# Recurrent block of a two-layer trunk: a result block's two halves are multiplied together, and two recurrence blocks stand ahead of the first gate pair

## The chip, the cores and the metric

The kernel runs on one core of one Trainium2 chip. The metric is the device time of one launch in microseconds (us). The engines are TensorE (PE: matrix products, into the accumulator memory PSUM), VectorE (DVE), ScalarE (ACT), GpSimd (POOL) and SyncE (SP), whose queue issues the transfers. Each engine works through its own list in order; semaphores tie the lists together.

## What is computed

A trunk of two layers over 1024 tokens of width 1024: a recurrent block and a squared-ReLU MLP, then a chunked attention and another MLP. The change touches only the recurrent block:

```python
def recurrent_block(x, w_in, conv_w, conv_b, w_gate, b_gate, lam, w_out):
    u = x @ w_in                          # x is already RMS-normed
    gate, rec = u[..., :D_RNN], u[..., D_RNN:]
    rec = causal_depthwise_conv(rec, conv_w, conv_b)     # 4 taps
    h = rg_lru(rec, w_gate, b_gate, lam)
    return (jax.nn.gelu(gate) * h) @ w_out

def rmsnorm(x, g):
    y = xf * lax.rsqrt(jnp.mean(xf * xf, axis=-1, keepdims=True) + EPS)
    return (y * g.astype(jnp.float32)).astype(x.dtype)
```

`rg_lru` makes, for each of 8 groups of 128 channels, two gates (`sigmoid` of a 128 x 128 product each), from them a factor `a` and an input `b` per token, and runs h[t] = a[t] h[t-1] + b[t] along the tokens.

## The kernel before

**Layout.** Everything is held with channels on the 128 partitions and tokens along the row: 8 blocks of 128 channels by 1024 tokens. A product is done as three matmuls of 128 x 128 by 128 x 512 (`mm`, lines 335 to 337), high and low parts of both operands: wh*xh, wh*xl, wl*xh. So one result block of 128 channels by 1024 tokens over 8 blocks of input is 8 x 2 halves x 3 = 48 matmuls. It fills a tile `p` of PSUM, 128 x 1024 in fp32, whose two halves of 512 tokens are called 0 and 1 (`hs(h)`). There are four such tiles (`bank2`, counted by `pss`).

**The norm** of the input isn't applied ahead of the product. The product runs over x times the gain, and the result is multiplied by the root of each token, `R[0]` and `R[1]`, one for each half. That is line 598, on VectorE, in place in PSUM.

**The blocks.** r(n) is the block n of the recurrence's input, g(n) that of the gate, p(n) the pair of 128 x 128 gate products of recurrence block n (12 matmuls into two tiles). r0 and g0 run together at the start; then `order` (line 473) says what PE does: "r1 g1 p0 r2 p1 r3 p2 g2 r4 p3 g3 r5 p4 g4 r6 p5 r7 g5 p6 g6 p7 g7". In a block (`block`, line 701) PE does half 0 and half 1 over the first four input blocks, then half 0 and half 1 over the last four. Behind w_in's blocks come those of w_out ("out").

**The chains.** What follows a block is written as a Python generator:

- `conv(n)`, line 604: multiplies done, it takes a buffer `c`, forms the last tap on ScalarE (line 611), adds the other three on VectorE (line 618) and lets the tile `p` go; then it takes two buffers and splits `c` into `ch` and `cl` (lines 627, 629), which p(n) reads. From n = 2 on it first waits for `posted[n - 2]`.
- `lru(n)`, line 633, behind p(n): takes three buffers and sets `posted[n]`, sigmoids of both tiles (lines 640, 642, which let them go), tanh, line 648 on GpSimd (which lets `c` go), exp and one minus on ScalarE (653, 654), lines 656 to 664 on VectorE, 666 on GpSimd, and the scan, line 670, which sets `hidden[n]`.
- `gate(n)`, line 677, behind g(n): a buffer of another kind, the GELU (line 682, which lets the tile go), times the hidden state (687), and a split into the operands of w_out (693, 695).
- `split_half`, line 486, makes the high and low part of half a weight block (493 on ScalarE, 495 on VectorE) in ten tiles `w`, counted by `wss`; the weights with places 2 and 3 in the sequence (`IN_G`) take tiles of another pool. `worder` is that sequence: r0, g0, and then `order` without the pairs.

Buffers `c`, `ch`, `cl` and those of `lru` are of one kind; there are seven (`bs`). Those of `gate` and the result of `lru` are of another; there are four (`xs`).

**What sets the order.** The program of all engines is written in the order that a small model of time, `Plan`, finds when it is built. `Plan.pe` adds 512 columns at 2260 per us to PE's time, `Plan.use` a cost to another engine's; a generator yields a time, a `Flag` or a `Sema` and goes on when the plan's time has come there. What a generator calls is emitted at that moment, so the plan decides in what sequence each engine gets its instructions. The waits between engines are put in afterwards, from which instruction writes and reads which tile.

**The step of the change.** When `block` has emitted the last product of a half (`k == ks[-1]`), it starts `scale(ps, h, done)` for that half; `scale` waits for `normal[h]`, emits line 598 for that half and sets `done[h]`. `conv` and `gate` begin with `yield done[0]` and `yield done[1]`.

Of the kernel before, what the change touches and what calls it, by code (L numbers as in the profile page):

```python
# [13 lines left out]
ALU = mybir.AluOpType  # L14
# [4 lines left out]
NF = 8  # L19
H2 = 512  # L20
# [18 lines left out]
LAT = 0.3  # L39
# [119 lines left out]
def tile_yoco_rglru_chunk_attention(  # L159
# [17 lines left out]
    act, dve, pool, pe = nc.scalar, nc.vector, nc.gpsimd, nc.tensor  # L177
# [20 lines left out]
    def nm(s):  # L198
        cnt[0] += 1
        return f"{s}_{cnt[0]}"  # L200
# [10 lines left out]
    def bf(s="b", dt=F32):  # L211
        return bp.tile([P, T], dt, tag="b", name=nm(s))
# [25 lines left out]
    def hs(h):  # L238
        return slice(h * H2, (h + 1) * H2)
# [161 lines left out]
    plan = Plan(2260)  # L401
    R = [None, None]
    X = [[None, None] for _ in range(NF)]
# [46 lines left out]
    def d_(n):  # L450
        return 0.16 + n * 0.00106
# [6 lines left out]
    def flags(*shape):  # L458
        return {x: Flag(plan) for x in itertools.product(*(range(n) for n in shape))}
# [3 lines left out]
    normal, gained = flags(2), flags(1)  # L463
# [6 lines left out]
    goods = Sema(plan, 0)  # L470


    order = "r1 g1 p0 r2 p1 r3 p2 g2 r4 p3 g3 r5 p4 g4 r6 p5 r7 g5 p6 g6 p7 g7".split()
    order = [(x[0], int(x[1])) for x in order]
    worder = [NF, 0] + [n + NF * (kind == "r") for kind, n in order if kind != "p"]
    wsrc = [w_in[x] for x in worder] + [w_out[j] for j in range(NF)]
# [115 lines left out]
        dve.scalar_tensor_tensor(lo, x, g, hi.bitcast(F32), ALU.mult, ALU.subtract)  # L592
        parted[k, h].set(plan.use("dve", d_(H2)))

    def scale(ps, h, done):
        yield plan.now + LAT
        yield normal[h,]
        dve.tensor_tensor(ps[:, hs(h)], ps[:, hs(h)], R[h], ALU.mult)  # L598
        done.set(plan.use("dve", d_(H2)))

    def scales(ps, h, done):
        plan.start(scale(ps, h, done[h]))

    def conv(n, ps, done):
        yield done[0]
        yield done[1]
        if n >= 2:
            yield posted[n - 2,]
        yield bs
        c = bf("c")  # L610
        act.activation(
            c, ps, AF.Identity,
            scale=vec[:, V_CW + 3, n : n + 1], bias=vec[:, V_CB, n : n + 1],
        )
        yield plan.use("act", a_(T))
        for k in range(3):
            d = 3 - k
            dve.scalar_tensor_tensor(
                c[:, d:], ps[:, : T - d], vec[:, V_CW + k, n : n + 1], c[:, d:], ALU.mult, ALU.add
            )  # L620
            yield plan.use("dve", d_(T)) - LAT
        pss.release(plan.t + LAT)
        yield plan.t + LAT
        yield bs
        yield bs
        ch, cl = bf("ch", F32R), bf("cl", F32R)
        act.activation(ch, c, AF.Copy)
        yield plan.use("act", a_(T))
        dve.tensor_tensor(cl, c, ch.bitcast(F32), ALU.subtract)
        C[n] = c, ch, cl  # L630
        conved[n,].set(plan.use("dve", d_(T)))
# [42 lines left out]
        HID[n] = u  # L674
        hidden[n,].set(last)

    def gate(n, ps, done):
        yield done[0]
        yield done[1]
        yield xs  # L680
        g = xf("ge")
        act.activation(g, ps, AF.Gelu_apprx_tanh)
        last = plan.use("act", a_(T) + TABLE)
        pss.release(last)
        yield last
        yield hidden[n,]
        dve.tensor_tensor(g, g, HID[n], ALU.mult)
        last = plan.use("dve", d_(T))
        xs.release(last)
        yield last  # L690
        for h in range(2):
            hi, lo = gr("h"), gr("l")
            act.activation(hi, g[:, hs(h)], AF.Copy)
            yield plan.use("act", a_(H2))
            dve.tensor_tensor(lo, g[:, hs(h)], hi.bitcast(F32), ALU.subtract)
            Y[n][h] = (hi, lo)
        last = plan.use("dve", 2 * d_(H2))
        xs.release(last)
        out_y[n,].set(last)

    def block(ps, i, Z, ks, start, stop, done=None):
        ys = [[k for k in ks if k // 4 == y] for y in range(2)]
        for h, k in [(h, k) for mine in ys for h in range(2) for k in mine]:
            y = k // 4
            yield weighed[i, y]
            if Z is Y:
                yield out_y[k,]
            w = W[i, y]
            mm(
                ps[:, hs(h)], (w[0][:, k % 4, :], w[1][:, k % 4, :]), Z[k][h],  # L710
                start and k == ks[0], stop and k == ks[-1],
            )
            yield plan.pe(3 * H2) - LAT
            if i not in IN_G and h == 1 and k == ys[y][-1] and k % 4 == 3:
                wss.release(plan.now)
                wss.release(plan.now)
            if done and k == ks[-1]:
                scales(ps, h, done)

    def tensor():  # L720
        dones = [[Flag(plan), Flag(plan)] for _ in range(2 * NF)]
        pss_ = []
        for x in range(2):
            yield pss
            pss_.append(bank2())
        for h in range(2):
            for k in range(NF):
                for x in range(2):
                    yield weighed[x, k // 4]
                    yield parted[k, h]  # L730
                    w = W[x, k // 4]
                    ps = pss_[x]
                    mm(ps[:, hs(h)], (w[0][:, k % 4, :], w[1][:, k % 4, :]), X[k][h], k == 0, k == NF - 1)
                    yield plan.pe(3 * H2) - LAT
                    if k == NF - 1:
                        scales(ps, h, dones[x])
        for _ in range(8):
            wss.release(plan.now)
        plan.start(conv(0, pss_[0], dones[0]))
        plan.start(gate(0, pss_[1], dones[1]))  # L740
        allk = range(NF)
        for kind, n in order:
            if kind == "p":
                yield conved[n,]
                yield pss
                yield pss
                pair = []
                for e in range(2):
                    ps = bank2()
                    pair.append(ps)  # L750
                    gw, (c, ch, cl) = GW[n], C[n]
                    for h in range(2):
                        mm(ps[:, hs(h)], (gw[0][:, e, :], gw[1][:, e, :]), (ch[:, hs(h)], cl[:, hs(h)]), True, True)
                        yield plan.pe(3 * H2) - LAT
                bs.release(plan.now)
                bs.release(plan.now)
                wss.release(plan.now)
                plan.start(lru(n, *pair))
                continue
            yield pss  # L760
            ps = bank2()
            i = widx[n + NF * (kind == "r")]
            yield from block(ps, i, X, allk, True, True, dones[i])
            plan.start((conv if kind == "r" else gate)(n, ps, dones[i]))
        for _ in range(NG - 4 * NF - 4):
            goods.release(plan.now)
        plan.start(ahead_weights())
        ahead = {}
        for j in range(2):
            yield pss  # L770
            ahead[j] = bank2()
            yield from block(ahead[j], widx["out", j], Y, range(NF - 2), True, False)
        for j in range(2):
            yield from block(ahead[j], widx["out", j], Y, range(NF - 2, NF - 1), False, False)
        for j in range(NF - 2):
            if j in ahead:
                ps = ahead[j]
                yield from block(ps, widx["out", j], Y, range(NF - 1, NF), False, True)
            else:
                yield pss  # L780
                ps = bank2()
                yield from block(ps, widx["out", j], Y, allk, True, True)
            plan.start(o1.result(j, ps))

        last = {}
        for j in (NF - 2, NF - 1):
            yield pss
            last[j] = bank2()
        for k in allk:
            for j, ps in last.items():  # L790
                i = widx["out", j]
                yield weighed[i, k // 4]
                w = W[i, k // 4]
                for h in range(2):
                    mm(
                        ps[:, hs(h)], (w[0][:, k % 4, :], w[1][:, k % 4, :]), Y[k][h],
                        k == 0, k == NF - 1,
                    )
                    yield plan.pe(3 * H2) - LAT
                if k % 4 == 3:  # L800
                    wss.release(plan.now)
                    wss.release(plan.now)
                if k == NF - 1:
                    plan.start(o1.result(j, ps))
            for _ in range(4):
                goods.release(plan.now)
# [527 lines left out]
    X, R = o2.XS, o2.rr  # L1334
# [6 lines left out]
    plan = Plan()  # L1341
# [365 lines left out]
    with tc.manual_schedule(engines=set(ENG)) if ENG else ExitStack():  # L1707
# [3 lines left out]
        while True:  # L1711
            plan.flush()
            if begun < len(units) and filled >= due[begun] and rows.free(plan.now):
                n = units[begun]
# [19 lines left out]
    for j in range(JP):  # L1734
        for h in range(2):
            ps = bank()
# [73 lines left out]
```

## Time and profile before

| | us |
|---|---|
| median of 3 runs | 2137.61 (2136.71 to 2138.93) |
| the profiled execution | 2139.37 |
| span of the profile, first to last instruction | 2137.6 |

The page's busy digits, 40 equal slices of 53.4 us each (9 is 90% or more):

```profile
PE   9899999999999999999999999989999999999999
DVE  7777868877777776747777877777787777777743
ACT  7766635434344545546666666764543444444631
POOL 3222202333210000126656666650133332000000
```

The recurrent block is in the first six slices, up to 324 us, where the last product with w_out ends. In rows of the order of time there stand the start in us, the duration in us, engine, line, operation, out<-in; in brackets the idle time of the engine before it and what ended it. A matmul's row lasts 0.39 us though the next one starts 0.23 us after it, since matmuls are pipelined.

### The profile page before, as it was taken

How to read it: one execution, taken by the hardware profiler on the slowest of the kernel's cores; microseconds unless marked ns; L12 is line 12 of the kernel's file. 1: busy time of each engine (PE TensorE's matmuls, PEld its weight loads, DVE VectorE, ACT ScalarE, POOL GpSimd, SP SyncE). 2: the span in 40 equal slices, each digit the busy share in tenths (PEclk: the TensorE clock that was granted, in tenths of full speed). 3: DMA queues.
4: the chain of work that ended last, by engine and by line, in shares of the span. 5: the costliest groups of instructions: out<-in, count | busy, mean ns of one | idle time of the engine just before them, and what ended most of it. 6: DMA issues, size and time to landing. Idle time of an engine off the chain costs nothing.

```text
span 2137.6 us, 29379 instructions
## 1 busy us (share of the span) xinstructions
PE 2090.3 (98%) x9756; PEld 1729.4 (81%) x9756; DVE 1555.8 (73%) x2593; ACT 1102.3 (52%) x1964; POOL 592.5 (28%) x536
## 2 busy tenths in 40 slices
PE   9899999999999999999999999989999999999999
PEld 7677787888888888887888888878778888888887
DVE  7777868877777776747777877777787777777743
ACT  7766635434344545546666666764543444444631
POOL 3222202333210000126656666650133332000000
PEclk9999999999999999999999999999999999999999
DMA  4011334544469774534323333343364445987733
GB/s 161 30 38 45 118 104 158 177 157 155 150 233 315 240 257 129 165 117 110 87 73 97 91 91 83 86 155 124 103 215 144 158 153 173 332 260 243 243 107 94
DMA packets 174296, 319.21 MB, mean 149 GB/s; under 512 B 20544, under 2 KB 22592, under 8 KB 174144
## 3 DMA queue, kind: packets, MB, share of 16 engines
q1 hardware_dynamic: 174144, 317.33, 46.0%
q8 instruction: 77, 1.26, 0.3%
q14 instruction: 75, 0.61, 0.1%
HBM read 219.73 MB, written 78.64 MB: 140 GB/s over the span
## 4 chain that ended last, share of the span: by engine, by line
PE 86%; DVE 7%; ACT 3%; issue 2%; DMA 1%; POOL 1%; SPq 0%; DVEq 0%; POOLq 0%; ACTq 0%
PE pj L335 11%; PE pj L337 11%; PE pj L336 11%; PE tp L335 6%; PE tp L337 6%; PE tp L336 6%; PE sc L336 4%; PE sc L337 4%; PE sc L335 4%; PE p L335 3%; PE p L336 3%; PE p L337 3%; PE tp L1591 2%; PE po L1619 2%; PE po L1618 1%
## 5 line engine op out<-in xcount | busy, mean ns | idle before, releaser
L335 PE MATMUL pj<-h,wh 128*128 128x512 f32 x1198 | 481.3, 402 | 4.8 <-DVE s L1126 3.5
L336 PE MATMUL pj<-l,wh 128*128 128x512 f32 x1198 | 467.6, 390 | 0.7 <-POOL l L1644 0.7
L337 PE MATMUL pj<-h,wl 128*128 128x512 f32 x1198 | 467.8, 391 | 0.2
L1045 ACT ACTIVATE wh<-raw 128x512 fp32r<-128x512 f32 x349 | 218.9, 629 | 316.7 <-PE po L336 86.1
L1046 DVE TENSOR_TENSOR wl<-raw,wh 128x512 fp32r<-128x512 f32 x349 | 269.9, 776 | 103.3 <-ACT wh L1045 99.7
L335 PEld LDWEIGHTS pj<-h,wh 128*128 128x128 f32 x1198 | 225.7, 188 | 48.4 <-DVE s L1126 4.5
L337 PEld LDWEIGHTS pj<-h,wl 128*128 128x128 f32 x1198 | 224.9, 188 | 49.2 <-DVE wl L1046 1.0
L336 PEld LDWEIGHTS pj<-l,wh 128*128 128x128 f32 x1198 | 225.9, 189 | 38.9 <-POOL l L1644 1.4
L335 PE MATMUL tp<-h,wh 128*128 128x512 f32 x569 | 221.5, 389 | 0.0
L336 PE MATMUL tp<-l,wh 128*128 128x512 f32 x569 | 221.4, 389 | 0.0
L337 PE MATMUL tp<-h,wl 128*128 128x512 f32 x569 | 221.4, 389 | 0.0
L349 DVE TENSOR_TENSOR l<-raw,h 128x512 fp32r<-128x512 f32 x224 | 153.9, 694 | 29.7 <-ACT h L348 28.3
L335 PE MATMUL p<-h,wh 128*128 128x512 f32 x384 | 153.7, 400 | 21.6 <-DVE p L598 21.0
L348 ACT ACTIVATE h<-raw 128x512 fp32r<-128x512 f32 x224 | 137.4, 620 | 58.0 <-DMA raw<-hid 34.8
L336 PE MATMUL sc<-l,wh 128*128 128x512 f32 x425 | 166.0, 391 | 0.0
L337 PE MATMUL sc<-h,wl 128*128 128x512 f32 x425 | 165.9, 391 | 0.0
L335 PE MATMUL sc<-h,wh 128*128 128x512 f32 x425 | 165.6, 390 | 0.0
L1127 ACT ACTIVATE s<-s 128x512 f32<-128x512 f32 x125 | 78.3, 629 | 164.7 <-DVE s L1126 164.7
L1054 POOL TENSOR_TENSOR raw<-raw,raw 128x512 f32<-128x512 f32 x30 | 49.7, 1658 | 407.0 <-DVE wl L1046 399.7
L336 PE MATMUL p<-l,wh 128*128 128x512 f32 x384 | 151.7, 395 | 0.3 <-DVE l L592 0.2
L337 PE MATMUL p<-h,wl 128*128 128x512 f32 x384 | 151.3, 394 | 0.1
L295 POOL TENSOR_TENSOR raw<-raw,vec 128x512 f32<-128x512 f32 x48 | 54.2, 1130 | 262.3 <-DVE l L349 259.2
(276 smaller groups left out, 4224.6 us busy)
## 6 DMA issues: line engine op xcount, KB each, us to landing
raw<-hid SPq DMA_DIRECT2D x224, 256.0 KB, 3.6
hid<-s SPq DMA_DIRECT2D x221, 256.0 KB, 2.1
raw<-in_w_down SPq DMA_DIRECT2D x192, 256.0 KB, 3.5
raw<-in_w_up SPq DMA_DIRECT2D x128, 256.0 KB, 2.6
s<-in_w_down SPq DMA_DIRECT2D x64, 256.0 KB, 4.4
raw<-in_w_in SPq DMA_DIRECT2D x32, 256.0 KB, 2.7
raw<-in_w_kv SPq DMA_DIRECT2D x32, 256.0 KB, 3.5
od<-ev SPq DMA_DIRECT2D x48, 128.0 KB, 2.2
```

What stands on the lines that cost most here:

```text
L295: pool.tensor_tensor(raw, raw, gains, ALU.mult)
L335: pe.matmul(ps, lhsT=wh, rhs=xh, start=start, stop=False, skip_group_check=more)
L336: pe.matmul(ps, lhsT=wh, rhs=xl, start=False, stop=False, skip_group_check=more)
L337: pe.matmul(ps, lhsT=wl, rhs=xh, start=False, stop=stop, skip_group_check=more)
L348: act.activation(h, src, AF.Copy)
L349: dve.tensor_tensor(l, src, h.bitcast(F32), ALU.subtract)
L1045: act.activation(wh, raw, AF.Copy)
L1046: dve.tensor_tensor(wl, raw, wh.bitcast(F32), ALU.subtract)
L1054: pool.tensor_tensor(raw[A11], raw[A11], raw[A21], ALU.add)
L1127: act.activation(out, out, AF.Square)
L1591: pe.transpose(pt[:, g * P : (g + 1) * P], sc[:, (kb - kb0) * P : (kb - kb0 + 1) * P], ident)
L1619: pe.matmul(out, lhsT=st, rhs=pl[:, off : off + wid], start=False, stop=y == final)
```

## The change

Two edits.

1. `order` begins "r1 r2 p0 g1 p1 r3" instead of "r1 g1 p0 r2 p1 r3"; the rest is as before.
2. `scale` is no longer started for each half from within `block`. It is a part of `conv` and `gate`, which are started when the whole block has been emitted, and emits line 598 for half 0 and half 1 one behind the other. In `conv` it stands behind the wait for `posted[n - 2]` and behind the taking of the buffer `c`. The flags `done` are gone.

```diff
-    order = "r1 g1 p0 r2 p1 r3 p2 g2 r4 p3 g3 r5 p4 g4 r6 p5 r7 g5 p6 g6 p7 g7".split()
+    order = "r1 r2 p0 g1 p1 r3 p2 g2 r4 p3 g3 r5 p4 g4 r6 p5 r7 g5 p6 g6 p7 g7".split()
...
-    def scale(ps, h, done):
+    def scale(ps):
         yield plan.now + LAT
-        yield normal[h,]
-        dve.tensor_tensor(ps[:, hs(h)], ps[:, hs(h)], R[h], ALU.mult)
-        done.set(plan.use("dve", d_(H2)))
-
-    def scales(ps, h, done):
-        plan.start(scale(ps, h, done[h]))
-
-    def conv(n, ps, done):
-        yield done[0]
-        yield done[1]
+        for h in range(2):
+            yield normal[h,]
+            dve.tensor_tensor(ps[:, hs(h)], ps[:, hs(h)], R[h], ALU.mult)
+            last = plan.use("dve", d_(H2))
+        yield last
+
+    def conv(n, ps):
+        yield plan.now + LAT
         if n >= 2:
             yield posted[n - 2,]
         yield bs
+        yield from scale(ps)
         c = bf("c")
...
-    def gate(n, ps, done):
-        yield done[0]
-        yield done[1]
+    def gate(n, ps):
+        yield from scale(ps)
         yield xs
         g = xf("ge")
...
-    def block(ps, i, Z, ks, start, stop, done=None):
+    def block(ps, i, Z, ks, start, stop):
...
-            if done and k == ks[-1]:
-                scales(ps, h, done)
...
-            yield from block(ps, i, X, allk, True, True, dones[i])
-            plan.start((conv if kind == "r" else gate)(n, ps, dones[i]))
+            yield from block(ps, i, X, allk, True, True)
+            plan.start((conv if kind == "r" else gate)(n, ps))
```

More of the change, by code (lines that the diff above doesn't have):

```diff
@@ L716, in block @@
                 wss.release(plan.now)
-            if done and k == ks[-1]:
-                scales(ps, h, done)
     def tensor():
-        dones = [[Flag(plan), Flag(plan)] for _ in range(2 * NF)]
         pss_ = []
@@ L734, in tensor @@
                     yield plan.pe(3 * H2) - LAT
-                    if k == NF - 1:
-                        scales(ps, h, dones[x])
         for _ in range(8):
             wss.release(plan.now)
-        plan.start(conv(0, pss_[0], dones[0]))
-        plan.start(gate(0, pss_[1], dones[1]))
+        plan.start(conv(0, pss_[0]))
+        plan.start(gate(0, pss_[1]))
         allk = range(NF)
```

## The prediction

> **What bounds the kernel now.** I read the busy shares first, then the busy time by stretch, then what TensorE (PE) waited for, then PE's instructions in order of time around those waits.
>
> ```profile
> PE 2090.3 (98%) x9756; PEld 1729.4 (81%) x9756; DVE 1555.8 (73%) x2593; ACT 1102.3 (52%) x1964; POOL 592.5 (28%) x536
> ```
> ```profile
> 36.00:242.00 206.00, 184.73 (x779) 147.51 (x778) 161.04 (x155) 142.48 (x152) 48.35 (x27) 0.98 0.15 49
> ```
> ```profile
> PE p L335 <- DVE p L598: 21.0, 14, 6.5
> PE p L336 <- DVE cl L629: 0.3, 1, 0.3
> ```
>
> PE is the bound of the whole. In the stretch from 36 to 242 us, where the fourteen blocks r1 to g7 and the eight gate pairs run, it is busy 184.73 of 206 us, and the list of waits says what the other 21 us are: 14 waits, one for each block, all for line 598, the multiplication by the root that the change moves.
>
> ```profile
> 43.38 0.50 PE L335 MATMUL p<-h,wh 128*128 128x512 f32 x1 [1.69 <-DVE p L598]
> ...
> 46.27 0.39 PE L335 MATMUL p<-h,wh 128*128 128x512 f32 x1
> ...
> 54.20 0.39 PE L337 MATMUL p<-h,wl 128*128 128x512 f32 x1
> 55.38 0.50 PE L335 MATMUL p<-h,wh 128*128 128x512 f32 x1 [0.79 <-DVE p L598]
> 55.72 0.39 PE L336 MATMUL p<-l,wh 128*128 128x512 f32 x1
> ...
> 57.56 0.39 PE L335 MATMUL p<-ch,gw 128*128 128x512 f32 x1
> ```
> ```profile
> 48.95 1.22 DVE L629 TENSOR_TENSOR cl<-c,ch 128x1024 fp32r<-128x1024 f32 x1
> ...
> 54.63 0.70 DVE L598 TENSOR_TENSOR p<-p,rneg 128x512 f32<-128x512 f32 x1 [1.95 <-PE p L337]
> ```
>
> The wait at 55.38 stands inside block g1: from it to the first matmul of p0 at 57.56 there is room for 9 of the block's 48 matmuls (2.18 us). So PE has done all of half 0 and one group of three of half 1 when it stops. VectorE (DVE) starts line 598 on half 0 at 54.63, when that group has ended, and PE goes on at 55.38, when DVE has ended. The two halves are different columns of one tile `p`; the program orders them by the tile. This ping-pong takes 0.79 us where DVE is free, and more where line 598 stands behind other work on DVE. The plan that writes the order (`plan.pe`) knows nothing of it.
>
> **The change part by part.** *What a wait costs.* The 35 steps from 46.27 to 54.20 take 7.93 us, 0.2267 each. From 54.20 to 55.38 are 1.18 us and from 55.38 to 55.72 another 0.34, which is 1.07 us more than two steps: a wait listed as 0.79 costs 0.28 more. Two long waits also slow the clock:
>
> ```profile
> 106.31 0.79 PE L335 MATMUL p<-h,wh 128*128 128x512 f32 x1 [6.53 <-DVE p L598]
> 106.90 0.63 PE L336 MATMUL p<-l,wh 128*128 128x512 f32 x1
> ...
> 111.59 0.42 PE L335 MATMUL p<-h,wh 128*128 128x512 f32 x1
> ```
> ```profile
> 232.97 0.50 PE L335 MATMUL p<-h,wh 128*128 128x512 f32 x1 [2.68 <-DVE p L598]
> ...
> 234.46 0.58 PE L335 MATMUL p<-h,wh 128*128 128x512 f32 x1
> ...
> 238.10 0.39 PE L335 MATMUL p<-h,wh 128*128 128x512 f32 x1
> ```
>
> 106.90 to 111.59 is 11 steps in 4.69 us against 2.49, with 0.25 for the slow first one: 2.45 lost. 234.46 to 238.10 is 9 steps in 3.64 against 2.04: 1.6 lost. [...]
>
> *Removed.* 21.0 listed, 0.3 for the wait on `cl`, 14 x 0.28 = 3.9 for the restarts, 2.45 + 1.6 for the clock: **29.3 us**. A check by another way: from 55.38 to 232.97 (the 40th matmul of g1 to that of g7) lie 12 blocks of 48 and 8 pairs of 12, 672 matmuls or 152.3 us; it took 177.6, so 25.3 are lost there, and the 1.97 of the wait at 43.38, 0.95 ahead of 55.38 and 1.7 behind 232.97 make 29.9.
>
> *Same work, later.* All 32 multiplications stay, 693 ns each; none is added. What changes is that half 0 of a block isn't done in the shadow of half 1: after a block's last matmul stand two instead of one, some 0.6 us more before the convolution or the GELU, and before the tile comes free. PE pays only if it wants that tile or that convolution sooner. In the loop a pair p(n) comes two blocks and one pair after r(n) (24.5 us of matmuls). The chain in between, by rows:
>
> ```profile
> L618 DVE SCALAR_TENSOR_TENSOR c<-p,vec,c 128x1021 f32<-128x1021 f32 (+2 forms) x24 | 30.5, 1272 | 4.8 <-ACT c L611 4.6
> L598 DVE TENSOR_TENSOR p<-p,rneg 128x512 f32<-128x512 f32 x32 | 22.0, 693 | 31.5 <-PE p L337 31.4
> L629 DVE TENSOR_TENSOR cl<-c,ch 128x1024 fp32r<-128x1024 f32 x8 | 10.1, 1259 | 5.5 <-ACT ch L627 5.5
> ```
>
> Two multiplications, two passes of ScalarE over 1024 columns (1.15 each, by line 654 below), three multiply-adds and the split: 2 x 0.69 + 2 x 1.15 + 3 x 1.27 + 1.26 = 8.8 us, so 15.7 us are left for queues. The same rows show what DVE gets back: it stood 31.4 us in line 598 waiting for PE, with all its other work queued behind. I cost this part at 0; without the cover it is 0.6 x 14 = 8.4 us.
>
> *The order.* r2 changes places with p0 and g1. Without its wait r1 ends at about 43.6 (its 40th matmul at 43.38 - 1.69 - 0.16, since a matmul's end lies 0.16 behind the next one's start, and 9 x 0.2267), r2 at 54.4, p0 at 57.2, g1 at 68.0, p1 at 70.8. The weights keep their places by number, so the loads on SP's queue and the splits behind them keep their sequence and number; only the block that the third and the fourth of them belong to is another. p0 needs line 629 of block 0, done at 50.2 (the row at 48.95). Two things get worse. First, four tiles `p` exist: at 70.8 two belong to p1, so r3 needs that of g1 or r2. g1's comes free after two multiplications (1.3) and a GELU (some 1.1, ScalarE's 1024 columns again), at 70.5 to 72. r2's is held long: `conv(2)` may start only when `lru(0)` has its buffers and a buffer `c` is free (after line 648, which runs while ScalarE is between the two lines shown first):
>
> ```profile
> 60.84 1.12 ACT L640 ACTIVATE sig<-p,vec 128x1024 f32<-128x1024 f32 x1
> ...
> 66.55 1.15 ACT L654 ACTIVATE sig<-sig,onesr 128x1024 f32<-128x1024 f32 x1
> ...
> 76.59 1.12 ACT L640 ACTIVATE sig<-p,vec 128x1024 f32<-128x1024 f32 x1
> ```
> ```profile
> 79.41 4.00 DVE L670 TENSOR_TENSOR_SCAN q<-sig,tanh 128x1024 f32<-128x1024 f32 x1
> ...
> 103.39 2.28 DVE L670 TENSOR_TENSOR_SCAN q<-sig,tanh 128x1024 f32<-128x1024 f32 x1
> ```
>
> The first pair's sigmoid comes some 3 us earlier (57.8), its line 654 ends at 64.6, and behind it the 1.15 + 3 x 1.27 of `conv(2)` with lines 656 to 664 in between end at 72 to 73.5. So r3 waits 0 to 2.7 us; I take 1.5, near the GELU, and 0.3 for the restart. Second, `ch` and `cl` of block 2 come only after the first scan, at about 80 (now the scan ends 22.6 us behind its sigmoid, 60.84 to 83.41; I take 20, since waits behind line 598 go and the other scan shown takes 2.28 instead of 4.00, and 2.4 for the two splits); p2 wants them at 83: 0 to 2, I take 0. Behind that the order is that of before.
>
> *What is late next.* At the end of the stage the last product of w_out wants gate(7)'s result 132 matmuls, 29.9 us, behind p7:
>
> ```profile
> 235.92 0.70 DVE L598 TENSOR_TENSOR p<-p,rneg 128x512 f32<-128x512 f32 x1 [2.42 <-PE p L337]
> 236.53 1.22 DVE L656 SCALAR_TENSOR_TENSOR q<-tanh,sig 128x1024 f32<-128x1024 f32 x1
> ...
> 251.61 1.29 DVE L695 TENSOR_TENSOR l<-ge,h 128x512 fp32r<-128x512 f32 x2
> ```
>
> Now p7 ends at 221.3 (the 40th matmul of g7 at 232.97, less 2.68, 0.16 and 39 x 0.2267) and that result at 252.9, 31.6 us later; 2.4 of it is line 656 standing behind line 598, which goes. 29.2 against 29.9: 0 to 2, I take 0.5. And DVE, 161 busy us in a stretch of 177 instead of 206, will be late here and there: a bound is the 0.79 that it costs now at each block, 14 x 0.79 = 11, the other end is 0; nearer to the one wait of 0.3 on `cl` than to that, I take 3.
>
> **Sum**: 29.3 - 1.8 - 0.5 - 3 = 24 us from the profiled execution's 2139.4 (span 2137.6), so 2115.4. The median of the runs shown is 1.8 us lower than that execution; **2113.6**.
>
> **The rivals.**
>
> *No new wait at all.* The plan no longer misjudges PE, so its order fits. All 29.3 come: 2137.6 - 29.3 = 2108.3. For it: the one wait of PE on the chain behind a block was 0.3. Against: r3's tile.
>
> *The wait is for buffers, and stays.* PE stands because tiles `p` are short, and the change, which adds none, moves the gap from inside the block to its edge, where the next tile is taken: 14 x (0.79 + 0.28) = 15 of the 29.3 remain, and 2137.6 - 14.3 = 2123.3. For it: the gap recurs at every block. Against: it stands at the 40th matmul of a block, where no tile is taken. [...]
>
> *The start clogs.* r2's early tile and `conv(2)` hold two of four tiles and the buffers; r3 waits 4 us, p2 as much, each long enough for the slow clock (2 x 2.45): 13 us with the smaller terms 3.5, 2137.6 - 12.8 = 2124.8.
>
> *The recurrence becomes the bound: slower.* From its sigmoid at 76.59 to the end of its scan at 105.67 block 1 takes 29.1 us. If buffers let only one recurrence be under way, the stage has a period of 29 to 30 us where PE needs 24.5 and now takes 28.2 (24.5 + 29.3/8). It decides above 28.2; at 30 it costs 8 x 1.8 = 14.4: 2152. For it: seven buffers, of which a recurrence takes three and a convolution three. Against: scans end at 83.4 and 105.7 now, 22 us apart, though each takes 29, so they overlap.
>
> **How the numbers follow.** Forecast 0.50, no new wait 0.22, gap at the edge 0.07, clogged start 0.13, recurrence 0.06, and 0.02 that gains and waits cancel. About 0.2% (4.3 us) is what a measurement can tell from no change. The first four are all faster: 0.92; same 0.02; slower 0.06. The range runs from below the full gain, 2107, to 2124, the forecast with all late terms at their upper ends (29.3 - 3 - 2 - 11 = 13.3).
>
> **What would show it.** Right: no row "PE p <- DVE p L598" inside a block; from r1 to g7 start to end about 768 x 0.2267 = 174 us plus a few; clock 1.00 from 100 to 120; a wait of 1 to 3 us before r3, for line 682 or 618. Wrong: waits on 618 or 682 at every block's first matmul (tiles), on `cl` line 629 at pairs (recurrence), on `l` line 695 ahead of the last w_out products, or a clock under 1 again.

## The result, and the profile after

The changed kernel takes **2115.06 us** (median of 4 runs, 2113.88 to 2116.18). The kernel before, beside it on the same chip, takes 2138.27 (median of 4, 2136.71 to 2139.79). The ratio is 0.9891 with a 95% interval of 0.9874 to 0.9909: faster by 23.2 us. The forecast was 2113.6. The profiled execution takes 2114.83 against 2139.37, and its span is 25.5 us shorter than before's 2137.6.

The first two rows of the page of the kernel after:

```profile
span 2112.1 us, 29367 instructions
PE 2082.3 (99%) x9756; PEld 1727.3 (82%) x9756; DVE 1561.5 (74%) x2593; ACT 1103.7 (52%) x1965; POOL 589.8 (28%) x536
```

PE, DVE and POOL have the same number of instructions as before, ACT one more. What went is idle time of PE. The busy time by stretch, of the kernel after, with the recurrent block's blocks and pairs in the first row and a part of its middle in the second:

```profile
36.00:218.00 182.00, 180.01 (x791) 147.98 (x790) 164.35 (x154) 140.85 (x149) 45.32 (x25) 1.00 0.17 55
...
100.00:120.00 20.00, 20.00 (x90) 16.56 (x89) 19.90 (x20) 16.65 (x19) 6.11 (x3) 1.00 0.14 47
```

PE is idle for 2.0 us of the 182, where before it was for 21 of 206, and its clock is 1.00. DVE is now busy for 164 of 182 us, and for 19.90 of 20 in the middle, yet there PE doesn't wait for it once. In the list of PE's waits the row for the multiplication (now line 599) is gone. Three other waits show, two at p2 and one where the next stage begins, in the rows of PE further below. The other lines of the chains have numbers 1 or 2 lower than in before, and what stands behind the blocks 7 lower: line 951, the addition of the residual, is 958 in before.

Where the time came from is seen by placing a few of PE's instructions of both kernels side by side. The kernel before, in order of time (row 1 is the sum for the norm ahead of the blocks, row 2 the last matmul with w_out, row 3 the first of the next stage):

```profile
19.99 1.02 PE L562 MATMUL p<-acc,onesr 128*128 128x512 f32 x2
...
323.57 0.39 PE L337 MATMUL p<-h,wl 128*128 128x512 f32 x1
323.80 0.39 PE L335 MATMUL pj<-h,wh 128*128 128x512 f32 x1
```

The kernel after, the same three points, and in between r3's first matmul and the start of p2:

```profile
19.40 1.02 PE L562 MATMUL p<-acc,onesr 128*128 128x512 f32 x2
...
70.20 0.50 PE L335 MATMUL p<-h,wh 128*128 128x512 f32 x1
...
81.97 0.50 PE L335 MATMUL p<-ch,gw 128*128 128x512 f32 x1 [0.60 <-ACT ch L626]
83.75 0.50 PE L336 MATMUL p<-cl,gw 128*128 128x512 f32 x1 [1.28 <-DVE cl L628]
...
296.06 0.39 PE L337 MATMUL p<-h,wl 128*128 128x512 f32 x1
298.14 0.50 PE L335 MATMUL pj<-h,wh 128*128 128x512 f32 x1 [1.69 <-DVE xr L951]
```

The last matmul with w_out comes 27.5 us earlier. 0.6 of it were there at the norm's sum already, ahead of the change (another execution of the changed kernel has that row at 19.97, so this is a difference between executions), so the blocks gave 26.9. The next stage then begins with a wait of 1.69 us that before doesn't have; with the restart that is 298.14 - 296.06 + 0.34 - 2 x 0.2267 = 2.0 us given back. 27.5 - 2.0 = 25.5, which is the whole difference of the spans. Behind that the distance between the two kernels changes by less than 1 us and ends where it was.

### The profile page after: what moved, and what is told of

It reads as the page before. It is cut to its first block, busy times and chain, and to the rows that moved or that the text cites. A ratio compares the mean times of both kernels' runs of the same rounds, so it can differ in the third digit from the quotient of the medians.

```text
span 2112.1 us, 29367 instructions
## 1 busy us (share of the span) xinstructions
PE 2082.3 (99%) x9756; PEld 1727.3 (82%) x9756; DVE 1561.5 (74%) x2593; ACT 1103.7 (52%) x1965; POOL 589.8 (28%) x536
## 3 DMA queue, kind: packets, MB, share of 16 engines
q8 instruction: 76, 1.25, 0.3%
## 4 chain that ended last, share of the span: by engine, by line
PE 90%; DVE 5%; DMA 2%; issue 2%; ACT 1%; POOL 1%; SPq 0%; DVEq 0%; POOLq 0%; ACTq 0%
PE pj L335 12%; PE pj L337 11%; PE pj L336 11%; PE tp L335 6%; PE tp L337 6%; PE tp L336 6%; PE sc L337 4%; PE sc L336 4%; PE sc L335 4%; PE p L336 4%; PE p L337 4%; PE p L335 4%; PE tp L1584 2%; PE po L1612 2%; PE po L1611 1%
## 5 line engine op out<-in xcount | busy, mean ns | idle before, releaser
L348 ACT ACTIVATE h<-raw 128x512 fp32r<-128x512 f32 x224 | 137.3, 620 | 57.8 <-DMA raw<-hid 35.0
```

Source lines behind the costliest of these rows:

```text
L348: act.activation(h, src, AF.Copy)
```

## The experiments

Theory: PE stood at the 40th matmul of each block because the multiplication of half 0 stands there in the program and both halves are one tile, and to move it behind the block is what pays. Rivals: the order pays (O); it is not the place in the block but how far the chains behind a block fall back (A, and others named with each run). Each ratio is to the kernel before, with its 95% interval, from runs on one chip.

### The order alone

```diff
 (before)
-    order = "r1 g1 p0 r2 p1 r3 p2 ..."
+    order = "r1 r2 p0 g1 p1 r3 p2 ..."
```

> Edit: before, with the new order alone (r1 r2 p0 g1 p1 r3); half 0 of each block is still multiplied while half 1 runs. Theory (PE waits since both halves are one tile, and the program puts the multiplication of half 0 behind the first group of half 1's last part): 14 waits for line 598 inside the blocks stay, eight or more of them 0.79 us; only the lengths that came from VectorE's queue (6.53, 1.28, 2.68) may change, so the time lies between 2128 and 2142 us. Rival (the order is what gains): about 2115 us and few waits for line 598.

2151.38 us, ratio 1.006 (1.0043 to 1.0077): **slower by 13.5**, outside what was expected. The list of waits and PE's order of time of this kernel:

```profile
PE p L335 <- DVE p L598: 20.8, 14, 4.6
```
```profile
80.83 0.76 PE L335 MATMUL p<-h,wh 128*128 128x512 f32 x1 [6.33 <-DVE c L618]
...
243.83 0.50 PE L335 MATMUL p<-h,wh 128*128 128x512 f32 x1 [2.69 <-DVE p L598]
...
245.32 0.39 PE L335 MATMUL p<-h,wh 128*128 128x512 f32 x1
...
334.90 0.50 PE L335 MATMUL pj<-h,wh 128*128 128x512 f32 x1 [1.69 <-DVE xr L958]
```

The fourteen waits on the multiplication stay whole (20.8 against 21.0), so O is refuted. A new one of 6.33 us stands at r3's first matmul: it wants the tile of r2, which line 618 still reads. The last row is the wait at the next stage, already seen in the kernel after: it belongs to the order. When that tile comes free shows on DVE of the same kernel:

```profile
68.69 0.70 DVE L598 TENSOR_TENSOR p<-p,rneg 128x512 f32<-128x512 f32 x1 [10.86 <-PE p L337]
69.30 1.22 DVE L656 SCALAR_TENSOR_TENSOR q<-tanh,sig 128x1024 f32<-128x1024 f32 x1
...
79.41 1.27 DVE L618 SCALAR_TENSOR_TENSOR c<-p,vec,c 128x1023 f32<-128x1023 f32 x1
```

Recurrence 0 could go on at 65.7, when line 654 ends on ACT (from 64.56 on, 1.15 us), but DVE stands for 10.86 us at a multiplication that waits for PE. So the recurrence runs 3.6 us late, `conv(2)` mixes with it, and r2's tile comes free at 80.7. That alone doesn't explain the wait: by the same line r2's tile comes free at 80.8 in the kernel after and at 84.6 in before, and there PE doesn't stop for it. What differs is that r3 was given r2's tile here, and g1's in the kernel after. Which of the four tiles a block is given can't be read from the trace, so why that is so stays open.

### The multiplication alone

```diff
 (after)
-    order = "r1 r2 p0 g1 p1 r3 p2 ..."
+    order = "r1 g1 p0 r2 p1 r3 p2 ..."
```

> Edit: after, with the old order (r1 g1 p0 r2 p1 r3). Theory: no wait for the multiplication inside a block, no clock under 0.98, and a time of 2110 to 2118 us; what the order adds is a wait or two at p1 or p2, up to 5 us. Rival (the order is what gains, or both are needed): over 2125 us, with long waits at pairs or at the first matmul of a block.

2118.28 us, ratio 0.9908 (0.9893 to 0.9923): 19.6 of the 23 us. The time, the waits at the pair (5.9 us) and the clock, which fell, all came out a little worse than expected. The difference to the kernel after, 3.2 us by the medians, lies within what the two intervals share, but the trace shows where it sits. PE at p2:

```profile
83.79 0.50 PE L335 MATMUL p<-ch,gw 128*128 128x512 f32 x1 [1.54 <-ACT ch L626]
...
88.69 0.80 PE L336 MATMUL p<-cl,gw 128*128 128x512 f32 x1 [4.40 <-DVE cl L628]
...
91.85 0.59 PE L337 MATMUL p<-ch,gw 128*128 128x512 f32 x1
```

With the old order p2 waits 1.54 + 4.40 instead of 0.60 + 1.28, 4.1 us more, and from 88.69 to 91.85, seven matmuls on, PE needs 3.16 us (steps of 0.42 to 0.60) instead of 7 x 0.2267 = 1.59 at the full clock, 1.6 more. The wait of 2.0 at the next stage is absent. 4.1 + 1.6 - 2.0 = 3.7; the spans differ by 5.0, and the rest lies ahead of the blocks (1.0 at the norm's sum) and in the stages behind. So the order is worth some 3 us **with** the moved multiplication and costs 13.5 **without** it: the two edits can't be priced apart and added.

### Both halves at the block's end, but not behind the convolution's waits

```diff
 (before)
-            if done and k == ks[-1]:
-                scales(ps, h, done)
+            if done and h == 1 and k == ks[-1]:
+                scales(ps, 0, done)
+                scales(ps, 1, done)
```

> Edit: before with its order and its flags, but both multiplications of a block are started when its last product has been emitted; conv and gate are otherwise as before, so the multiplications do not wait for posted or for a buffer. Theory: like the scale edit alone, 2110 to 2120 us, no wait for line 598 inside a block. Rival A (it matters that the multiplication stands behind the waits of conv): over 2122 us. Rival B (the equal gaps are for room, and move to the block's edge): 14 waits of about 0.8 us at the first matmul of the blocks, 2123 us.

2130.46 us, ratio 0.9965 (0.9951 to 0.9978). The waits on line 598 are gone, as the theory said, yet only 7.4 us are gained: the theory's time was missed and that of A held. The list of waits between 36 and 230 us of this kernel, and then two rows of ACT:

```profile
PE p L335 <- ACT ch L627: 14.4, 1, 14.4
PE p L336 <- DVE cl L629: 2.6, 1, 2.6
```
```profile
70.68 1.12 ACT L640 ACTIVATE sig<-p,vec 128x1024 f32<-128x1024 f32 x1
...
78.22 1.19 ACT L611 ACTIVATE c<-p,vec 128x1024 f32<-128x1024 f32 x1
```

Recurrence 1's sigmoid stands ahead of block 2's convolution on ACT. In the kernel with the multiplication alone, which has the same order, it is the other way about: block 2's convolution (line 610) starts on ACT at 70.22 and recurrence 1's sigmoid (line 639) at 73.56.

What differs is when `conv` asks for its buffer: in the change before the multiplication, here after it, and by then `lru(1)` has asked.

### The same, with the buffer asked for first

```diff
 (the kernel above)
     def conv(n, ps, done):
-        yield done[0]
-        yield done[1]
         if n >= 2:
             yield posted[n - 2,]
         yield bs
+        yield done[0]
+        yield done[1]
         c = bf("c")
```

> Edit: the kernel of e3_late (both multiplications started at the block's end, old order, flags), but conv asks for posted and for its buffer c ahead of the two flags instead of behind them, as after does. Theory (in e3_late lru(1) asked for its three buffers ahead of conv(2), so conv(2) stood behind the whole of recurrence 1): line 611 of block 2 stands ahead of line 640 of recurrence 1 again, the wait of 14.4 us at p2 shrinks to that of e2_scale (1.5 and 4.4), and the time is 2116 to 2121 us. Rival (the 14.4 us come from the multiplication standing too early in VectorE's queue): the wait stays over 10 us and the time near 2130.

2118.29 us, ratio 0.9908 (0.9893 to 0.9923): as the theory said, 12.2 us better than without, and equal to the multiplication alone. ACT of this kernel:

```profile
69.00 1.21 ACT L611 ACTIVATE c<-p,vec 128x1024 f32<-128x1024 f32 x1 [0.55 <-DVE p L598]
...
72.34 1.12 ACT L640 ACTIVATE sig<-p,vec 128x1024 f32<-128x1024 f32 x1
```

The waits at p2 fall to 3.8 and 2.8. So of the change's second edit not only the place in the block counts. That the `yield`s for `posted` and for the buffer stand **ahead** of the multiplication is worth 12 us with the old order; the two were not tried apart.

### Half 0 two products later

```diff
 (before)
-            if done and k == ks[-1]:
-                scales(ps, h, done)
+            if done and h == 1 and k == ks[-3]:
+                scales(ps, 0, done)
+            if done and h == 1 and k == ks[-1]:
+                scales(ps, 1, done)
```

> Edit: before, with the multiplication of half 0 started two products of half 1 later (behind its sixth input block instead of at its end of half 0), that of half 1 as before. Theory (the wait follows the place that the multiplication has in the program): still about 14 waits for line 598 of 0.79 us or more inside the blocks, but ahead of the 46th matmul instead of the 40th, and 2128 to 2140 us. Rival B (room): the waits do not move with the multiplication, or vanish.

2143.68 us, ratio 1.0027 (1.0018 to 1.0036), a little above what was expected. PE of this kernel, at the end of g1 and at that of g7:

```profile
55.55 0.50 PE L335 MATMUL p<-h,wh 128*128 128x512 f32 x1 [0.79 <-DVE p L598]
...
56.35 0.39 PE L335 MATMUL p<-ch,gw 128*128 128x512 f32 x1
...
237.99 0.50 PE L335 MATMUL p<-h,wh 128*128 128x512 f32 x1 [2.39 <-DVE p L598]
...
238.83 0.63 PE L335 MATMUL p<-h,wh 128*128 128x512 f32 x1
...
242.19 0.39 PE L337 MATMUL p<-h,wl 128*128 128x512 f32 x1
```

The same wait of 0.79 us now stands three matmuls ahead of p0, at the 46th of the block instead of the 40th. **It follows the place of the multiplication in the program**, two products of three matmuls later; a lack of tiles, or of weights, would not move with it. That the waits fell from 21.0 to 16.1 us brought nothing, since p2 waits 4.1 + 4.6 us here.

### The first product of the next stage last

```diff
 (after)
         z, v, y = bank("pj"), bank("sc"), bank("tp")
-        for ps, n, w in ((z, 0, a11), (v, 1, a12), (y, 4, s1)):
+        for ps, n, w in ((v, 1, a12), (y, 4, s1), (z, 0, a11)):
```

> Edit: after, with the first three products of the MLP in another order (v, y, z instead of z, v, y), so that the tile pj, whose place in PSUM the last result of w_out held, is written 18 matmuls (4.1 us) later. Theory (pj lies on the place of the last result, and its wait of 1.69 us at 298.1 for line 951 is for that alone): the wait is gone, the time is 2.0 us lower than after, about 2113 us. Rival (v or y lie there as well, or the wait is for the operands): a wait of 1 us or more stays at the first of the three, and the time is that of after.

2111.59 us (2110.30 to 2114.30), ratio 0.9879 (0.9864 to 0.9893). PE starts that stage at 297.27, now with the tile `sc`, and has no wait there. The wait on line 951 is gone, and one of 1.28 us comes new at 326.77, for another chain. Since the gain was within the intervals, both kernels were run again side by side:

> The changed kernel itself, unchanged, beside the next one on one chip: 2115 us, the wait of 1.7 us at the first matmul of the MLP in its profile.

> The kernel of e5_zlast once more, beside the changed kernel. Theory (the wait of 1.69 and its restart of 0.3 are gone and nothing takes their place): 2 us below the changed kernel, 0.9990 of it. Rival (e5_zlast's 3.5 us were spread between batches, and a later wait takes it back): the same time within 0.5 us.

The change again: 2115.28 (2113.74 to 2115.65), ratio 0.9896 (0.988 to 0.9913). With the product last: 2112.76 (2111.43 to 2113.87), ratio 0.9886 (0.9871 to 0.9901). So 2.5 us by the medians, twice in the same direction, with single runs that overlap by 0.13; **the best version found**, ahead of both kernels. It takes the wait away by letting the tile that needs the late place come last. That the wait is what gained the 2.5 us is not shown: "nothing takes their place" failed, since the new wait (1.27 here) takes most of it back. At 330 us the two profiles of this pair are only 0.4 us apart, of 2.6 at the end (spans of 2113.0 and 2110.4). What the other 2.2 are is not shown. In the first profile of this version the span is 2112.5, no shorter than the changed kernel's 2112.1. That this place is a bank that a result of w_out held is what the row of line 951 suggests; the trace doesn't give the place of a tile.

### Pairs later

In the version just shown, p2 behind g2, and then every pair from p2 to p6 one block later:

```diff
 (the version above)
-    order = "r1 r2 p0 g1 p1 r3 p2 g2 r4 p3 g3 r5 p4 g4 r6 p5 r7 g5 p6 g6 p7 g7"
+    order = "r1 r2 p0 g1 p1 r3 g2 p2 r4 p3 g3 r5 p4 g4 r6 p5 r7 g5 p6 g6 p7 g7"
```

> Edit: e5_zlast, and p2 stands behind g2 instead of ahead of it (r3 g2 p2 r4). Theory (p2 comes some 2 us before block 2's split is ready): the waits of 0.60 and 1.28 at p2 go, another 2.4 us, about 2110.5 us, if nothing behind it is late. Rival (recurrence 2 starts 11 us later, and what hangs on it, the buffers of conv(4) and p3, is late): new waits for line 628, 617 or 680 between 95 and 150 us, 2113 us or more.

```diff
 (the version above)
+    order = "r1 r2 p0 g1 p1 r3 g2 p2 r4 g3 p3 r5 g4 p4 r6 g5 p5 r7 p6 g6 p7 g7"
```

> Edit: e5_zlast with every pair from p2 on one block later (r3 g2 p2 r4 g3 p3 r5 g4 p4 r6 g5 p5 r7 p6 g6 p7 g7). Theory (e7_p2_later lost since p2 and p3 came to stand one block apart, with the two recurrences crowded): with two blocks between pairs again no wait at p2 and none behind, about 2109 to 2111 us. Rival (a later recurrence holds its buffers and keeps the next convolution and its tile waiting whatever the spacing): waits for line 617 or 628 of 2 us and more between 95 and 200 us, over 2114 us.

2117.63 us, ratio 0.9908 (0.9891 to 0.9924), and 2122.31, ratio 0.9932 (0.9918 to 0.9947): both worse than what they start from. The times are those of the rivals; the waits only in part. With p2 alone later the waits at p2 go, and three others come, at 96.2 us for line 639, at 159.1 for 628 and at 188.8 for 617, two of them later than the rival had them. The longest, PE of that kernel:

```profile
159.12 0.50 PE L336 MATMUL p<-cl,gw 128*128 128x512 f32 x1 [2.52 <-DVE cl L628]
159.46 0.40 PE L337 MATMUL p<-ch,gw 128*128 128x512 f32 x1
```

And with all the pairs later, where three of five new waits are for the sigmoids (lines 639 and 641):

```profile
123.40 0.47 PE L335 MATMUL p<-h,wh 128*128 128x512 f32 x1 [2.23 <-ACT sig L641]
...
123.94 0.54 PE L337 MATMUL p<-h,wl 128*128 128x512 f32 x1
...
127.58 0.39 PE L337 MATMUL p<-h,wl 128*128 128x512 f32 x1
```

A later pair holds its two tiles later, and the next block waits until the sigmoids let them go. Neither of these two shifts gains the 1.9 us at p2.

Not tried: two tiles instead of one for the halves, which would show whether half 0 can be multiplied in half 1's shadow with no wait at all.

## Why the prediction was right, step by step

| step | predicted, us | measured, us |
|---|---|---|
| waits, restarts and clock removed | 29.3 | 30.0 |
| r3's wait for a tile | -1.8 | -0.1 |
| p2's wait for block 2 | 0 | -2.4 |
| end of the stage, gate(7) | -0.5 | 0 |
| DVE late here and there | -3 | -0.5 |
| start of the next stage | not foreseen | -2.0 |
| sum | 24.0 | 24.9 |

The removal is counted in before itself: from 40.62 to 238.56 us (the 36th matmul of r1 to the 9th with w_out) PE makes 741 steps, which at 0.2267 are 168.0 us; they took 197.9, so 30.0 were lost. In the kernel after the same steps, from 40.02 to 211.06, lose 3.1: 2.4 at p2, 0.1 at r3, 0.4 in one short stop at 184.6, and the rest scattered. The terms are rounded. With the 0.6 us ahead of the change, 24.9 is the spans' 25.5.

- **What bounds the kernel, and what the wait is: right.** The wait was PE's against the multiplication's place, by the tile. Half 0 moved by two products moved it to the 46th matmul; both halves at the end removed it, in every kernel that does so. So the rival of the buffers falls: the tiles are still four, and in the kernel after PE has no listed wait at a block's edge.
- **The same work, later, at no cost: right.** Half 0's multiplication out of the shadow of half 1 lengthens each chain, and in the stretch from 100 to 120 PE lost nothing by it.
- **r3's tile: bounds right, value too high.** The tile was g1's, whose GELU ended in time for r3's 70.20 (line 680 on ACT of the kernel after, from 69.12 to 70.15).

- **p2: the step that failed.** I put `cl` of block 2 at about 80 and p2 at 83. p2 came at 81.4, since r3 didn't wait, and `cl` ended at 83.7. DVE of the kernel after, and then POOL:

```profile
64.19 1.22 DVE L656 SCALAR_TENSOR_TENSOR q<-q,sig 128x1024 f32<-128x1024 f32 x1
67.65 1.43 DVE L599 TENSOR_TENSOR p<-p,rneg 128x512 f32<-128x512 f32 x2 [2.23 <-PE p L337]
68.99 0.68 DVE L661 TENSOR_SCALAR sig<-q 128x1024 f32<-128x1024 f32 x1
...
71.92 2.01 DVE L495 TENSOR_TENSOR wl<-raw,wh 128x512 fp32r<-128x512 f32 x1
73.85 1.27 DVE L617 SCALAR_TENSOR_TENSOR c<-p,vec,c 128x1022 f32<-128x1022 f32 x1
75.05 2.40 DVE L495 TENSOR_TENSOR wl<-raw,wh 128x512 fp32r<-128x512 f32 x1
77.37 2.28 DVE L669 TENSOR_TENSOR_SCAN q<-sig,tanh 128x1024 f32<-128x1024 f32 x1
79.57 1.25 DVE L617 SCALAR_TENSOR_TENSOR c<-p,vec,c 128x1023 f32<-128x1023 f32 x1
...
82.48 1.21 DVE L628 TENSOR_TENSOR cl<-c,ch 128x1024 fp32r<-128x1024 f32 x1
```
```profile
70.98 2.40 POOL L665 TENSOR_TENSOR tanh<-tanh,sig 128x1024 f32<-128x1024 f32 x1 [10.34 <-DVE tanh L663]
...
74.49 2.41 POOL L647 TENSOR_TENSOR sig<-sig,c 128x1024 f32<-128x1024 f32 x1
```

What failed is the term of 20 us from recurrence 0's first sigmoid to the end of its scan, taken "since waits behind line 598 go". The sigmoid came earlier than foreseen (line 639 on ACT at 56.03, not 57.8), and yet the scan ended at 79.65, not at 77.8: 23.6 us, more than the 22.6 of before (the scan itself took the 2.28 that was assumed). The convolution's third multiply-add, and `ch` and `cl` after it, stood behind the scan. Two things made the stretch long. First, the wait behind the multiplication didn't go: line 656 ended at 65.41, but line 661, which reads its result, came at 68.99, since line 599 for g1 stood between them in DVE's queue, waited 2.23 us for PE and took 1.43. Second, two splits of weights stood ahead of the scan. They took 2.01 and 2.40 us where one with no work of GpSimd beside it takes 0.68 (at 81.88); each began while an operation of GpSimd was under way and ended 0.55 us behind that operation's end (73.93 against 73.38, 77.45 against 76.90). The multiply-add at 73.85, which reads one operand in PSUM, kept its 1.27 through the same time. The other rows of the two traces agree. Of the 96 rows of line 495 in the kernels before and after, 17 began while GpSimd was at line 539, 647 or 665 (539, 648 or 666 in before): one, 0.01 us behind that operation's start, took 0.69 us, and the other 16 took 0.94 to 2.90 and ended 0.55 us behind the operation. The remaining 79 took 0.66 to 0.69, and the 48 rows of the multiply-add 1.25 to 1.28 with and without GpSimd. What the two engines share isn't shown. By an estimate from these rows 2.01 + 2.40 - 2 x 0.68 = 3.05 us of the queue were GpSimd's. `cl` came 2.3 us after PE wanted it, so either of the two, 3.6 and 3.05 us, is enough for the waits at p2. Both are worked out from the rows; no run takes one of them away.
- **DVE late here and there: mis-sized.** At 90% busy it was late only at p2; all else that PE lost is 0.5 us.
- **The end of the stage: not late at gate(7)**, but 2.0 us were lost one step further, at a place where I had not looked. The wait of 1.69 us is in the change and in the kernel with the order alone, and in none of the five with the old order (before, the multiplication alone, and the three that place it otherwise). The order edit brought it.
- **The order edit's worth** was taken as about -1.8 for r3. With the moved multiplication it gains some 3 us; alone it loses 13.5.

The median came out 1.5 us above the forecast, though the trace's sum, 24.9, is larger than the 24.0 foreseen: the runs differ by that much among themselves (2113.88 to 2116.18). That both are so near is in part luck, since 5.3 us of losses were foreseen and 5.0 found, mostly elsewhere. Of the rivals, that of no new wait came out 6.8 us low, 5.0 of them by these losses. The clogged start had r3 and p2 each wait 4 us; together they waited 1.9. The recurrence never became the bound.

## What to carry to other kernels

An in-place operation on one half of a tile, written into the program while the other half is still being filled, was a wait for both engines here (21.0 us of PE, 31.4 of DVE): look for equal gaps at the same matmul number, and move the operation to see whether the gap goes with it. When such a wait goes, the queues behind it are rearranged, so price an edit to the order together with it, and read where a buffer is asked for as closely as where the work is done. Count what a queue holds with the durations it will have beside GpSimd (a split of weights took 2.01 and 2.40 us there, 0.68 without), and look at the first instructions of the next stage too.

## What the runs showed of the hardware

**The clock doesn't fall by the length of an idle gap alone.** Gaps of PE of 2.23 us (all pairs later), 2.39 (half 0 two products later) and 2.68 (before) were followed by slow matmuls, two to six matmuls after PE had started again; the rows are above and in the prediction. Gaps of 2.52 (p2 later) and 2.69 (order alone) were not: the matmuls behind them keep 0.39 to 0.40. The slow stretch is about the same each time, from 238.83 to 242.19 and from 123.94 to 127.58, 3.4 to 3.6 us. In the trace of before the granted clock itself is at half speed from 234.50 to 237.91, 3.413 us behind the gap of 2.68, and at the gap of 6.53 from 104.79 to 111.62, twice as long.

In these traces it goes by how the idle time lies on a grid. In before and after the granted clock changes only at whole multiples of 3.4133 us from its first change (in before at 104.79, then 111.62, 234.50, 237.91 and on to 2135.72). On this grid the two waits at p2 fall differently in two executions. Below are the windows around p2 in the second run with the product last (first two rows; waits of 0.59 and 1.27 us) and in the kernel after (last two; 0.60 and 1.28). A row has the window, its length, the busy time of PE, PEld, DVE, ACT and POOL, and then the granted clock:

```profile
81.57:84.98 3.41, 1.54 (x6) 0.97 (x6) 3.38 (x5) 3.35 (x4) 0.00 (x0) 1.00 0.23 74
84.98:88.39 3.41, 3.41 (x10) 2.63 (x9) 2.82 (x3) 3.38 (x5) 0.94 (x1) 0.50 0.03 8
```
```profile
79.68:83.10 3.42, 2.19 (x9) 1.26 (x7) 3.42 (x4) 2.23 (x2) 0.00 (x0) 1.00 0.06 20
83.10:86.51 3.41, 2.76 (x12) 2.27 (x13) 2.81 (x4) 3.35 (x6) 0.04 (x1) 1.00 0.28 82
```

In the first both waits lie in one window, which is idle for 1.87 us, and the next window runs at half clock. In the second they lie in two, idle for 1.23 and 0.65, and the clock stays. With each run's grid laid through its rows at half speed, the same holds for the gaps above: 2.23 and 2.39 lie whole in one window and 2.68 for 1.88 of it, but 2.52 is divided into 0.98 and 1.55, and 2.69 into 1.54 and 1.15. In the traces of before and after, from about 5 to 2104 us, 1223 windows run at full clock. None of the 1216 with under 1.78 us of idle time is followed by one at half; each of the four with 1.87 us or more is; of the three in between (1.78, 1.81 and 1.82) two are. So two short waits close together, 0.59 and 1.27 us, cost as much clock as the one of 2.68: a window at half.
